# All tile arithmetic of GpSimd moved to VectorE in a planned transformer kernel

## The chip, the cores and the metric

The kernel runs on one core of one Trainium2 chip. The metric is the time of one execution in microseconds, the median of several executions; lower is better. A core has five engines that run side by side, each with its own queue of instructions in a fixed order: TensorE (PE, matrix products; its weight loads are shown apart as PEld), VectorE (DVE), ScalarE (ACT), GpSimd (POOL) and SyncE (SP, which here only issues transfers). They meet through semaphores alone.

## What is computed

Two layers over 512 tokens of width 1024, everything in float32. `rms` is a root-mean-square norm with a gain; each half layer is normed before and after ("sandwich").

```python
# layer 0
m = conformer_conv(rms(h))        # 1024 -> 2048, gate, causal depthwise conv of 31 taps,
                                  # layer norm, silu, 1024 -> 1024
h = h + rms(m)
h = h + rms(square(relu(rms(h) @ w_ff1)) @ w_ff2)       # 1024 -> 4096 -> 1024
# keys and values, once, from h
c_kv = rms(rms(h) @ w_dkv)                              # 256 wide
k_rope = rope(rms(h) @ w_kr)                            # 64 wide, shared by the heads
k_nope, v = c_kv @ w_uk, c_kv @ w_uv                    # 8 heads of 128
# layer 1
q = rms(rms(h) @ w_dq) @ w_uq                           # 384 wide -> 8 heads of 128 + 64
p = softmax((q_nope @ k_nope.T + rope(q_rope) @ k_rope.T) * scale + mask)   # chunks of 64
h = h + rms((p @ v) @ w_o)
h = h + rms(square(relu(rms(h) @ w_ff1)) @ w_ff2)
```

## The kernel before, in words

**Products in three parts.** The matrix products keep float32 accuracy with a rounded type. Each operand X is split into a main part `hi`, a rounded copy made by ScalarE, and a remainder `lo = X - hi`; a product is hi*hi + lo*hi + hi*lo. The remainder is one subtraction of two tiles. `split` does both steps, for weights (from tile `raw` into `wh` and `wl`) and for activations (into two tiles `big`). Some weights get their remainder by an accumulating transfer that GpSimd issues instead (`lo_by_dma`).

**Fast matrix algorithms.** The feed-forward parts use Winograd's and Strassen's forms with seven products in place of eight. `combinations` prepares what the seven products of the first matrix need: it first adds `hi` and `lo` of every half of the normed activations back together (16 additions of 128x256 a layer), then forms differences of them, then splits those again.

**Attention.** For every head: `keys`, `queries`, and for every pair of heads `values` and `rotary` project the latents with weights `uk`, `uq`, `uv`, `uqr` (those and `wo` are called `ATT`; their splits are listed in `VG`, that is, VectorE or GpSimd). `rotate` applies the rotary embedding: four copies by ScalarE, a product with the cosines on VectorE, then a product with the sines and a sum on GpSimd (and a further scaling for the key's part). `scores` does the products of queries and keys for one half of the query blocks, then on VectorE a masked maximum, on ScalarE the exponential with its sum, on VectorE a reciprocal and the scaling; `transposed` transposes the result on TensorE and splits it; `attend` multiplies by the values. TensorE's order runs one head ahead: while head n is attended, the projections and scores of head n+1 are issued (`PROJECTIONS` says which projections go after which half head).

**The planner.** No instruction is issued directly. `record` collects operations with the ways each may be done (an engine, a method, a price in ns from `cost`). TensorE's order is the order of the program text; for the others `due` works back from the end when each operation must be done, `schedule` simulates the engines and takes on each the operation that is due first among those that are ready, choosing between engines where an operation has several ways (`better`), and `replay` times the finished order once more. Sixteen rounds are tried and the shortest is issued, by `issue`, so in the profile nearly every instruction has the line L786 and is told from others by its tiles. The planner also knows a port: an operation marked `port` (two-input arithmetic of GpSimd, or of VectorE with more than one input outside PSUM) is not begun while another such is being done.

**Where a planned gap of TensorE is long, it inserts idle products** (`mm<-ident`, `bc<-ident`).

**GpSimd's work** is thus: memsets, the issue of accumulating and some other transfers, and the tile arithmetic that the change below moves. It has 233 instructions.

Of the kernel before, what the change touches and what calls it, by code (L numbers as in the profile page):

```python
# [8 lines left out]
F32 = mybir.dt.float32  # L9
F32R = mybir.dt.float32r  # L10
AF = mybir.ActivationFunctionType
ALU = mybir.AluOpType
# [11 lines left out]
H = 256  # L24
# [247 lines left out]


PORT = ("tensor_tensor", "scalar_tensor_tensor")

LEAD = 16000.0

# [46 lines left out]
class Program:  # L324
# [15 lines left out]
    def record(self, *ways):  # L340
        op = Op(len(self.ops))
        op.early = self.early
        self.ops.append(op)
        for engine, method, args, kwargs in ways:
            outs, ins = [], []
            for i, a in enumerate(args):
                if isinstance(a, View):
                    (outs if i == 0 else ins).append(a)
            for k, a in kwargs.items():
                if isinstance(a, View):  # L350
                    (outs if k in ("out", "accum_out") else ins).append(a)
            aps = [self.model(v) for v in outs], [self.model(v) for v in ins]
            if not op.ways:
                for write, views in ((False, ins), (True, outs)):
                    for view, ap in zip(views, aps[0 if write else 1]):
                        psum = ap.tensor.space == PSUM
                        self.touch(op, view.tile, write, _box(ap, ap.tensor.space != bass.MemoryType.SB), psum and engine)
            wide = [a for a in aps[1] if a.tensor.space != PSUM]
            op.port = method in PORT and engine in VG and (engine == "gpsimd" or len(wide) > 1)
            op.ways.append((engine, method, args, kwargs, self.cost(engine, method, kwargs, *aps), op.port))  # L360
        op.choose(op.ways[0])
        if op.method == "dma_start":
            self.flight(op)
        return op
# [28 lines left out]
    def cost(self, engine, method, kwargs, outs, ins):  # L393
        n = max([_size(a) for a in outs + ins] or [1])
        if method == "dma_start":
            return {"scalar": 380.0, "gpsimd": 900.0}.get(engine, 400.0)
        apart = {"vector": 0.77, "scalar": 0.6}.get(engine, 0.0) * n if any(
            list(a.ap)[-1][0] > 1 for a in outs + ins if _size(a) > 8
        ) else 0.0
        if engine in ("scalar", "vector") and ins and _size(ins[0]) > 8 and ins[0].ap[0][1] < P:  # L400
            apart += 120.0 if engine == "scalar" else 97.0
        if engine == "tensor":
            n = _size(outs[0])
            if ins[0].dtype == F32R:
                k = ins[0].ap[0][1]
                return max(120.0, n / 2.4 + 13.7) + (200.0 if k < P else 0.0)
            return 109.0 if method == "transpose" else max(222.0, n / 0.6 + 9)
        few = sum(_size(a) == 1 for a in ins) if n > 8 else 0
        psum = any(a.tensor.space == PSUM for a in outs + ins)
        if engine == "vector":  # L410
            wide = [a for a in ins if _size(a) > 1]
            rate = 1.042 if len(wide) > 1 or psum else 0.521
            return 68 + rate * n + 62 * few + apart
        if engine == "scalar" and n == 1:

            return 1350.0
        if engine == "scalar":
            few += "accum_out" in kwargs
            return (51 if psum else 94) + 0.833 * n + 93 * few + apart
        if engine == "gpsimd" and not ins:  # L420
            return 97 + 0.85 * n
        if engine == "gpsimd" and method == "affine_select":
            return 182 + 0.85 * n
        if engine == "gpsimd":
            return 150 + 2.1 * n
        return 450.0

    def flight(self, op):
# [236 lines left out]
    def replay(self, sequence, pace=1.0, add=0.0):  # L665
# [23 lines left out]
                for p in op.deps:  # L689
                    p.heirs.append(op)  # L690
        clock = dict.fromkeys(ENGINES, 570.0)
        port = 0.0
        coming, rings, since = [], {"sync": deque(), "scalar": deque(), "gpsimd": deque()}, 0.0

        def finish(op, at):
# [7 lines left out]
        while left or coming or any(rings.values()):  # L703
            best = None
            for e in ENGINES:
                if queue[e]:
                    op, way = queue[e][0]
                    if op is None:
                        t = clock[e]
                    elif op.open:  # L710
                        continue
                    else:
                        t = max(clock[e], op.free, port if way[5] else 0.0)
                    if best is None or t < best[0]:
                        best = t, e
            heads = [r[0] for r in rings.values() if r]
            turn = sum(j[2] for j in heads)
            done = since + min(j[1] for j in heads) * turn if heads else None
            come = coming[0][0] if coming else None
            event = min((x for x in (done, come) if x is not None), default=None)  # L720
            if event is not None and (best is None or event <= best[0]):
                for j in heads:
                    j[1] -= (event - since) / turn
                since = event
                for r in rings.values():
                    while r and r[0][1] < 1e-6:
                        j = r.popleft()
                        finish(j[0], event + LANDS[j[0].engine])
                while coming and coming[0][0] <= event:
                    _, _, e, j = heappop(coming)  # L730
                    rings[e].append(j)
                continue
            if best is None:
                raise RuntimeError("no order")
            now, e = best
            op, way = queue[e].popleft()
            left -= 1
            if op is None:
                clock[e] = now + FILL
                continue  # L740
            op.real = now
            clock[e] = now + way[4] * (1.88 if e == "tensor" and now < COLD else 1.0)
            if way[5]:
                port = clock[e]
            if "dma" in way[1]:
                heappush(coming, (now + STARTS[e], op.n, e, [op, op.packets, op.serve * pace + add]))
            else:
                finish(op, clock[e])
# [41 lines left out]
def trunk(ctx: ExitStack, tc: tile.TileContext, xT, xN, wts, vec, along, rope, cw, out):  # L790
# [123 lines left out]
    def weight(key):  # L914

        while key not in blocks:
# [23 lines left out]
            if i >= 4 and lo_by_dma(name):  # L940

                for o in range(0, n, 512):
                    for dst, scale in ((lo, -1.0), (hi, 1.0)):
                        nc.scalar.activation(dst[:, o : o + 512], raw[:, o : o + 512], AF.Copy, scale=scale)
                nc.gpsimd.dma_start(out=lo, in_=src, accum_op=ALU.add)
            else:
                step = 256 if i < 2 else min(n, 512)
                engines = VG if name[0] in ATT else ("vector",)
                for o in range(0, n, step):
                    split(raw, slice(o, o + step), (hi, lo), engines=engines)  # L950
            blocks[name] = hi, lo
# [197 lines left out]
    def combinations(X):  # L1149

        raw = {}
        for kh, th in QUADS:
            for kp in range(2):
                a = raw[kh, th, kp] = big()
                for j in range(2):
                    hi, lo = (x[:, th * H : (th + 1) * H].bitcast(F32) for x in X[4 * kh + 2 * kp + j])
                    nc.binary(("gpsimd", "vector"), out=a[:, j * H : (j + 1) * H], in0=hi, in1=lo, op=ALU.add)
        out = {p: [] for p in WINOGRAD}
        for k, (hi, lo) in enumerate(X):
            out[1 if k < 4 else 2].append((hi[:, :H], lo[:, :H]))  # L1160
# [513 lines left out]
    def rotate(pt, n, s, r=None):  # L1674
# [4 lines left out]
                nc.scalar.activation(b[x : x + 32, s], pt[y : y + 32, :n], AF.Copy)  # L1679
        rc, rs = (rope_c, rope_s) if r is None else (rope_cd, rope_sd)  # L1680
        nc.vector.tensor_tensor(out=a[:, s], in0=pt[:, :n], in1=rc[:, s], op=ALU.mult)
        nc.gpsimd.tensor_tensor(out=b[:, s], in0=b[:, s], in1=rs[:, s], op=ALU.mult)
        nc.gpsimd.tensor_tensor(out=a[:, s], in0=a[:, s], in1=b[:, s], op=ALU.add)
        if r is not None:
            nc.gpsimd.tensor_tensor(out=a[:, s], in0=a[:, s], in1=r[:, s], op=ALU.mult)
        return a


# [2 lines left out]
    def query_latent(m, t):  # L1691
# [8 lines left out]
        if m == 0:  # L1700
            nc.scalar.activation(undealt(qsq, t), src, AF.Square)
        else:
            sq = tmp()
            nc.scalar.activation(undealt(sq, t), src, AF.Square)
            qs = undealt(qsq, t)
            nc.binary(VG, out=qs, in0=qs, in1=undealt(sq, t), op=ALU.add)

    for t in (HA, HB):
        s = slice(t[0], t[0] + t[1])
# [47 lines left out]
    def rotary(pr):  # L1757

        a = rotate(products(("uqr", pr), CQ, 0, T, nk=3), T, ALL)
        for j in range(2):  # L1760
            q = QR[2 * pr + j] = big(F32R)
            mine, other = slice(64 * j, 64 * j + 64), slice(64 - 64 * j, 128 - 64 * j)
            nc.scalar.activation(q[mine], a[mine], AF.Copy)
            nc.binary(VG, out=q[other], in0=a[mine], in1=q[mine].bitcast(F32), op=ALU.subtract)

    def keys(hd):
        KN[hd] = pair()
# [225 lines left out]
```

## Time and profile before

| | |
|---|---|
| median of 3 executions | 1054.61 us (1054.33 to 1054.73) |
| the profiled execution | 1054.81 us, span 1052.6 us |
| TensorE busy, granted clock | 1032.1 us (98%), 0.997 |
| VectorE busy | 852.9 us (81%) |
| ScalarE busy | 679.0 us (65%) |
| GpSimd busy | 190.8 us (18%), its transfer issues included |

Times run from the first instruction of the span. A row of the grouped instructions gives line, engine, operation, output <- inputs, shape, count | busy us, mean ns of one | the engine's idle time ahead of them and who ended it. A row of the waits gives the waiting engine and tile, the one that released it, the total in us, the number of waits and the longest. A row of the timeline gives start, duration, engine, operation and, in brackets, the idle time before it. A row by stage gives the stretch, its length, then busy time and count of PE, PEld, DVE, ACT and POOL, the granted clock, the share of the transfer engines and GB/s. Matmul records overlap, as they are pipelined.

The stages by time: convolution layer to about 180 us, then the turn to the first feed-forward part (180 to 215), that part to about 535, latents and first projections to 567, the heads to 665, the output projection to 715, the turn to the second feed-forward part (715 to 740), and that part to the end.

### The profile page before, as it was taken

How to read it: one execution, taken by the hardware profiler on the slowest of the kernel's cores; microseconds unless marked ns; L12 is line 12 of the kernel's file. 1: busy time of each engine (PE TensorE's matmuls, PEld its weight loads, DVE VectorE, ACT ScalarE, POOL GpSimd, SP SyncE). 2: the span in 40 equal slices, each digit the busy share in tenths (PEclk: the TensorE clock that was granted, in tenths of full speed). 3: DMA queues.
4: the chain of work that ended last, by engine and by line, in shares of the span. 5: the costliest groups of instructions: out<-in, count | busy, mean ns of one | idle time of the engine just before them, and what ended most of it. 6: DMA issues, size and time to landing. Idle time of an engine off the chain costs nothing.

```text
span 1052.6 us, 16355 instructions
## 1 busy us (share of the span) xinstructions
PE 1032.1 (98%) x5750; PEld 897.3 (85%) x5750; DVE 852.9 (81%) x1657; ACT 679.0 (65%) x1351; POOL 190.8 (18%) x233
## 2 busy tenths in 40 slices
PE   8999999999999999999999999999999999999995
PEld 7888988899988888888898888889999878888884
DVE  6599994798999648859988977648989895497798
ACT  9462795877875546465767777558778764555652
POOL 1123201501011010101015443315010110000010
PEclk9999999999999999999999999999999999999998
DMA  9996997657899976769423210956588998766782
GB/s 321 308 230 174 355 291 180 140 140 172 269 280 295 268 200 204 193 182 251 99 86 102 66 68 1 347 153 141 141 205 262 297 298 258 195 200 166 209 211 80
DMA packets 67794, 211.50 MB, mean 201 GB/s; under 512 B 7936, under 2 KB 11648, under 8 KB 67712
## 3 DMA queue, kind: packets, MB, share of 16 engines
q1 hardware_dynamic: 50688, 151.20, 41.1%
q0 software_dynamic: 16304, 58.20, 29.4%
q10 hardware_dynamic: 720, 1.05, 0.3%
q8 instruction: 45, 0.74, 0.3%
q14 instruction: 37, 0.30, 0.1%
HBM read 204.92 MB, written 5.51 MB: 200 GB/s over the span
## 4 chain that ended last, share of the span: by engine, by line
PE 62%; DVE 14%; ACT 4%; issue 2%; DMA 0%; DVEq 0%; ACTq 0%
PE mm L786 61%; DVE big L786 8%; DVE wl L786 3%; PE bc L786 2%; ACT big L786 2%; DVE stat L786 1%; ACT wh L786 1%; DVE tmp L786 1%; ACT junk L786 1%; DVE raw L786 1%; DVE h L786 1%; DMA raw<-wts 0%; ACT wl L786 0%; ACT tmp L786 0%; DVEq L1989 0%
## 5 line engine op out<-in xcount | busy, mean ns | idle before, releaser
L786 PE MATMUL mm<-big,wh 128*128 128x256 f32 (+1 forms) x1800 | 442.0, 335 | 1.6 <-DVE big L786 1.1
L786 PE MATMUL mm<-wh,big 128*128 128x512 f32 (+1 forms) x1216 | 372.3, 385 | 0.0
L786 PEld LDWEIGHTS mm<-big,wh 128*128 128x128 f32 x1800 | 308.2, 190 | 36.4 <-ACT wh L786 1.7
L786 ACT ACTIVATE wh<-raw 128x512 fp32r<-128x512 f32 (+3 forms) x430 | 266.1, 663 | 77.0 <-PE mm L786 48.0
L786 PE MATMUL mm<-big,wl 128*128 128x256 f32 (+1 forms) x900 | 301.3, 336 | 0.6 <-DVE wl L786 0.5
L786 DVE TENSOR_TENSOR wl<-raw,wh 128x512 fp32r<-128x512 f32 (+3 forms) x335 | 234.5, 737 | 51.8 <-ACT wh L786 51.7
L786 PEld LDWEIGHTS mm<-wh,big 128*128 128x128 f32 x1216 | 226.0, 188 | 43.9 <-ACT wh L786 0.2
L786 PE MATMUL mm<-wl,big 128*128 128x512 f32 (+1 forms) x608 | 233.5, 385 | 1.1 <-DVE wl L786 1.1
L786 PEld LDWEIGHTS mm<-big,wl 128*128 128x128 f32 x900 | 170.8, 190 | 18.2 <-DVE wl L786 1.7
L786 DVE TENSOR_TENSOR big<-big,big 128x512 f32<-128x512 f32 (+4 forms) x167 | 109.0, 672 | 56.1 <-ACT big L786 37.8
L786 PEld LDWEIGHTS mm<-wl,big 128*128 128x128 f32 x608 | 114.2, 188 | 25.3 <-DVE wl L786 2.9
L786 POOL DMA_DIRECT2D raw<-wts x64 | 56.2, 883 | 428.9 <-DMA raw<-wts 134.3
L786 ACT ACTIVATE big<-tmp 128x512 fp32r<-128x512 f32 (+2 forms) x152 | 76.4, 525 | 56.0 <-DVE tmp L786 45.5
L786 ACT ACTIVATE big<-big 128x512 f32<-128x512 f32 (+4 forms) x152 | 83.3, 574 | 15.8 <-DVE big L786 13.1
L786 ACT ACTIVATE big<-mm 128x512 f32<-128x512 f32 (+5 forms) x126 | 64.8, 520 | 37.7 <-PE mm L786 35.9
L786 PE MATMUL mm<-big,big 128*128 128x256 f32 (+3 forms) x520 | 84.4, 310 | 0.5 <-ACT big L786 0.2
L786 PEld LDWEIGHTS mm<-big,big 128*128 128x128 f32 x520 | 72.8, 190 | 5.7 <-ACT big L786 1.2
L786 DVE TENSOR_TENSOR big<-big,mm 128x512 f32<-128x512 f32 x102 | 67.4, 682 | 11.4 <-PE mm L786 11.2
L786 POOL DMA_DIRECT2D wl<-wts x42 | 36.6, 872 | 218.5 <-ACT wl L786 189.1
L786 DVE TENSOR_TENSOR big<-tmp,big 128x512 fp32r<-128x512 f32 (+1 forms) x104 | 64.5, 624 | 6.5 <-ACT big L786 3.1
L786 ACT ACTIVATE tmp<-mm 128x512 f32<-128x512 f32 (+1 forms) x41 | 25.0, 609 | 68.5 <-PE mm L786 67.3
L786 DVE SCALAR_TENSOR_TENSOR big<-big,vt,big 128x512 fp32r<-128x512 f32 (+29 forms) x95 | 63.1, 731 | 5.6 <-ACT big L786 5.3
(93 smaller groups left out, 894.7 us busy)
## 6 DMA issues: line engine op xcount, KB each, us to landing
raw<-wts SPq DMA_DIRECT2D x224, 512.0 KB, 6.0
raw<-wts POOLq DMA_DIRECT2D x64, 512.0 KB, 8.7
wl<-wts POOLq DMA_DIRECT2D x42, 512.0 KB, 8.6
big<-cw SPq DMA_DIRECT2D x45, 256.0 KB, 6.5
big<-wts SPq DMA_DIRECT2D x12, 256.0 KB, 2.6
big<-along SPq DMA_DIRECT2D x10, 256.0 KB, 5.7
raw<-wts SPq DMA_DIRECT2D x12, 192.0 KB, 2.8
big<-xT SPq DMA_DIRECT2D x8, 256.0 KB, 4.4
```

What stands on the lines that cost most here:

```text
L786: return f(*args, **kwargs)
```

## The change

Every operation on tiles that GpSimd did or could do is given to VectorE alone: the additions in `combinations`, the remainders of attention weights in `weight`, the products and sums of `rotate`, the sum of squares in `query_latent` and the remainder of the rotated queries in `rotary`. The planner's prices for GpSimd, its rule of the port (which instructions hold it, and that a wait is only due when the other engine holds it) are changed as well.

```diff
+FAST = ("tensor_scalar", "tensor_copy")
...
             op.port = method in PORT and engine in VG and (engine == "gpsimd" or len(wide) > 1)
+            op.port |= method in FAST and engine == "vector" and len(wide) == len(aps[1]) and _size(aps[0][0]) > 64
...
         if engine == "gpsimd":
-            return 150 + 2.1 * n
+            return 235 + 2.2 * n
...
-        port = 0.0
+        port, held = 0.0, None
...
-                        t = max(clock[e], op.free, port if way[5] else 0.0)
+                        t = max(clock[e], op.free)
+                        if way[5] and held != e:
+                            t = max(t, port + 40.0 * (e == "vector"))
...
             if way[5]:
-                port = clock[e]
+                port, held = clock[e], e
...
-                engines = VG if name[0] in ATT else ("vector",)
+                engines = ("vector",)
...
-                    nc.binary(("gpsimd", "vector"), out=a[:, j * H : (j + 1) * H], in0=hi, in1=lo, op=ALU.add)
+                    nc.binary(("vector",), out=a[:, j * H : (j + 1) * H], in0=hi, in1=lo, op=ALU.add)
...
-        nc.gpsimd.tensor_tensor(out=b[:, s], in0=b[:, s], in1=rs[:, s], op=ALU.mult)
-        nc.gpsimd.tensor_tensor(out=a[:, s], in0=a[:, s], in1=b[:, s], op=ALU.add)
+        nc.vector.tensor_tensor(out=b[:, s], in0=b[:, s], in1=rs[:, s], op=ALU.mult)
+        nc.vector.tensor_tensor(out=a[:, s], in0=a[:, s], in1=b[:, s], op=ALU.add)
         if r is not None:
-            nc.gpsimd.tensor_tensor(out=a[:, s], in0=a[:, s], in1=r[:, s], op=ALU.mult)
+            nc.vector.tensor_tensor(out=a[:, s], in0=a[:, s], in1=r[:, s], op=ALU.mult)
...
-            nc.binary(VG, out=qs, in0=qs, in1=undealt(sq, t), op=ALU.add)
+            nc.binary(("vector",), out=qs, in0=qs, in1=undealt(sq, t), op=ALU.add)
...
-            nc.binary(VG, out=q[other], in0=a[mine], in1=q[mine].bitcast(F32), op=ALU.subtract)
+            nc.binary(("vector",), out=q[other], in0=a[mine], in1=q[mine].bitcast(F32), op=ALU.subtract)
```

## Prediction

> **What bounds the kernel now.** I read the page's first part, then the busy times by stage, then who waited for whom on the weight loads of TensorE, then the timeline where it waits.
>
> ```profile
> PE 1032.1 (98%) x5750; PEld 897.3 (85%) x5750; DVE 852.9 (81%) x1657; ACT 679.0 (65%) x1351; POOL 190.8 (18%) x233
> ```
>
> TensorE is the bound: 20.5 of 1052.6 us idle. The profiled execution took 1054.81 us (its span and 2.2 us around it), 0.2 us over the median of the runs, 1054.61; sums are made against 1054.8. A measurement of this kernel tells about 0.2% (2.1 us) from no change.
>
> Two answers by stage follow: the turns between layers (180 to 215 and 715 to 740), a stage of pure matrix products (215 to 340), attention over the heads (567 to 665.5), the output projection (665.5 to 715), and the end.
>
> ```profile
> 180.00:215.00 35.00, 33.64 (x243) 31.24 (x242) 28.50 (x61) 25.37 (x57) 15.25 (x19) 1.00 0.47 106
> 215.00:340.00 125.00, 125.00 (x804) 114.36 (x803) 116.41 (x187) 95.36 (x165) 16.45 (x19) 1.00 0.85 236
> ...
> 567.00:665.50 98.50, 95.16 (x566) 82.79 (x565) 82.29 (x241) 75.08 (x172) 38.65 (x34) 1.00 0.19 59
> 665.50:715.00 49.50, 49.50 (x239) 40.98 (x238) 23.81 (x48) 28.52 (x60) 12.03 (x12) 1.00 0.68 227
> 715.00:740.00 25.00, 24.68 (x207) 24.47 (x206) 23.95 (x52) 19.47 (x45) 11.18 (x16) 1.00 0.59 142
> ...
> 989.00:1040.00 51.00, 51.00 (x227) 42.23 (x226) 50.84 (x102) 28.00 (x57) 4.74 (x6) 1.00 0.65 171
> 1040.00:1052.60 12.60, 1.89 (x9) 1.23 (x7) 9.05 (x31) 1.63 (x4) 0.00 (x0) 0.75 0.33 125
> ```
>
> The columns are length, PE, PEld, DVE, ACT, POOL. PE has no gap in the long product stages, though VectorE is 93% busy there (116.4 of 125). Its gaps lie at the turns and in attention, which are the places where GpSimd computes. So a gain or a loss can only come from those; the end from 989 us on holds no tile arithmetic of GpSimd and moves along unchanged.
>
> Who ended the waits of the weight loads, by stage (attention; turn of layer 0; turn of layer 1). I take these rows for PE's stalls, since the ends of the matmuls themselves are modelled and hide part of a gap.
>
> ```profile
> PEld bc L786 <- DVE big L786: 4.5, 8, 0.8
> PEld bc L786 <- issue: 1.2, 1, 1.2
> ...
> PEld mm L786 <- DVE big L786: 1.3, 1, 1.3
> PEld bc L786 <- issue: 0.7, 2, 0.4
> ...
> PEld bc L786 <- issue: 0.5, 1, 0.5
> ```
>
> Attention 5.7 us, the turns 2.0 and 0.5. Why VectorE is late there shows in the timeline, once at the turn and once in attention:
>
> ```profile
> 190.22 3.13 POOL L786 TENSOR_TENSOR big<-big,big 128x256 f32<-128x256 f32 x4
> 191.68 2.23 DVE L786 TENSOR_TENSOR big<-big,big 128x512 f32<-128x512 f32 x1
> 194.96 0.30 PEld L786 LDWEIGHTS mm<-big,wh 128*128 128x128 f32 x2 [1.29 <-DVE big L786]
> ...
> 610.97 1.41 POOL L786 TENSOR_TENSOR big<-big,big 128x512 f32<-128x512 f32 x1
> 611.38 1.29 DVE L786 TENSOR_SCALAR big<-big,stat 128x512 f32<-128x512 f32 x1
> 612.72 0.20 PEld L786 LDWEIGHTS bc<-ident,big 128*128 128x128 f32 x2 [0.73 <-DVE big L786]
> ...
> 598.32 0.49 DVE L786 TENSOR_SCALAR big<-big,stat 128x512 f32<-128x512 f32 x1
> ```
>
> The same softmax scaling lasts 0.49 us alone and 1.29 us when a GpSimd instruction began before it; it ends when GpSimd does, and TensorE waits 0.73 us for it. The rows of the tiles say it of more instructions: minimum, median and maximum are
>
> ```profile
> L786 DVE SCALAR_TENSOR_TENSOR h<-big,stat,h x32: 740/746/2820, 182.9 to 1048.6; 128x512 f32<-128x512 f32 x32
> ...
> L786 DVE TENSOR_SCALAR big<-big,stat x32: 262/421/1461, 586.4 to 667.6; 128x128 f32<-128x128 f32 x8, 128x256 f32<-128x256 f32 x8, 128x384 f32<-128x384 f32 x8, 128x512 f32<-128x512 f32 x8
> ```
>
> **The change part by part.** It removes GpSimd's tile arithmetic and adds the same instructions to VectorE's queue. GpSimd keeps its DMA issues and memsets. The edits of the planner's prices and port rule have nothing left to act on, since every instruction that holds the port is then VectorE's own; but the planner searches the whole order anew, so instructions far from attention can also change places.
>
> *Price of one moved instruction.* What VectorE takes for the shapes in question:
>
> ```profile
> L786 DVE TENSOR_TENSOR big<-mm,big 128x256 fp32r<-128x256 f32 x16 | 6.3, 418 | 0.7 <-ACT big L786 0.6
> ...
> L786 DVE TENSOR_TENSOR big<-bc,big 128x384 fp32r<-128x384 f32 x16 | 8.7, 548 | 1.5 <-ACT big L786 1.4
> ...
> 478.85 1.20 DVE wl L786 x2
> ```
>
> In the chain two 512-wide remainders follow each other in 1.20 us, 0.60 apart; one alone lasts 0.685, so 0.08 overlaps with the next. I take 0.60, 0.47 and 0.34 us for 512, 384 and 256 columns.
>
> *The turns.* At 180 to 215 GpSimd does 15 sums of the convolution's halves for the Winograd-like combinations:
>
> ```profile
> L786 POOL TENSOR_TENSOR big<-big,big 128x256 f32<-128x256 f32 x15 | 12.6, 981 | 3.2 <-DVE big L786 1.6 <-DVE stat L786 1.5
> ```
>
> On VectorE 15 x 0.34 = 5.1 us. Against it stand the holds: the first add above 2.23 instead of 0.69, the longest of `h` 2.82 instead of 0.75; these two alone give 3.6 us back. VectorE's load, 28.5 of 35, thus rises by 1.5 us at most, and may fall. TensorE's stalls here go with their cause: 1.3 + 0.7. The turn of layer 1 has the same sums once more and 0.5. Together -2.2 us (0.3 of 2.5 kept as what is late next: the residual adds wait for ACT's sums of squares anyway). Bounds: -2.5 if all goes, 0 if the sums, now in VectorE's own queue, delay the adds as GpSimd did.
>
> *Attention.* What moves there:
>
> ```profile
> L786 POOL TENSOR_TENSOR big<-big,big 128x512 f32<-128x512 f32 x8 | 10.9, 1362 | 27.0 <-ACT big L786 26.7
> L786 POOL TENSOR_TENSOR wl<-raw,wh 128x512 fp32r<-128x512 f32 x7 | 9.1, 1309 | 12.7 <-ACT wh L786 10.3 <-issue 2.4
> L786 POOL TENSOR_TENSOR wl<-raw,wh 128x384 fp32r<-128x384 f32 x8 | 8.1, 1013 | 5.3 <-ACT wh L786 4.4 <-PE mm L786 0.8
> L786 POOL TENSOR_TENSOR big<-big,big 64x512 fp32r<-64x512 f32 x5 | 6.4, 1286 | 4.0 <-ACT big L786 2.8 <-issue 1.2
> L786 POOL TENSOR_TENSOR wl<-raw,wh 128x256 fp32r<-128x256 f32 x6 | 4.4, 736 | 7.5 <-ACT wh L786 5.3 <-PE bc L786 2.2
> ```
>
> 20 instructions of 512 columns x 0.60 + 8 x 0.47 + 6 x 0.34 = 17.8 us more for VectorE. What it gets back are the holds, by the stage's own rows:
>
> ```profile
> L786 DVE TENSOR_SCALAR big<-big,stat 128x512 f32<-128x512 f32 x7 | 5.5, 785 | 0.2
> ...
> L786 DVE TENSOR_SCALAR big<-big,stat 128x256 f32<-128x256 f32 x7 | 4.0, 570 | 0.1
> L786 DVE TENSOR_SCALAR big<-big,stat 128x384 f32<-128x384 f32 x7 | 3.9, 551 | 0.2
> L786 DVE TENSOR_SCALAR big<-big,stat 128x128 f32<-128x128 f32 x8 | 3.3, 408 | 0.2
> ...
> 582.11 1.41 DVE L786 SCALAR_TENSOR_TENSOR stat<-stat 128x4 f32<-128x4 f32 x2
> ```
>
> Free of holds, the smallest takes 0.262 (the minimum above) and the largest 0.49; between them 0.34 and 0.41. So 7 x 0.295 + 7 x 0.23 + 7 x 0.14 + 8 x 0.146 = 5.8, and 1.1 for the two tiny steps at 582 us (1.41 instead of two of 0.16): 6.9 us. VectorE then needs 82.3 + 17.8 - 6.9 = 93.2 us in a stage of 98.5, and TensorE 98.5 - 5.7 = 92.8. They come out level: VectorE joins TensorE as a bound. The stage's length is 93.2 divided by the share of it in which VectorE manages to work. Two rows bound that share: 93% (215 to 340) gives 100.2, a loss of 1.7; 99.7% (50.84 of 51, 989 to 1040) gives 93.5, a gain of 5.0. Neither is nearer in kind: attention has shorter dependencies than the first, less backlog than the second. I take the middle, 96.4%: 96.7, a gain of 1.8. What helps is that weight remainders are not urgent and can fill VectorE's gaps; what hurts is VectorE's queue in order: the idle columns of the rows above show some 50 us in which GpSimd sat waiting for ACT's first half, at no cost. On VectorE such a wait would stop the softmax steps queued behind it, for which TensorE waits.
>
> *The rest.* Before and after the heads' stage:
>
> ```profile
> 535.00:567.00 32.00, 32.00 (x240) 30.41 (x239) 26.04 (x66) 19.49 (x42) 13.38 (x13) 1.00 0.39 122
> ```
>
> ```profile
> L786 POOL TENSOR_TENSOR wl<-raw,wh 128x512 fp32r<-128x512 f32 x5 | 7.3, 1460 | 24.7 <-ACT wh L786 10.8 <-PE mm L786 7.9 <-DMA raw<-wts 5.9
> ```
>
> At 535 to 567 there are 13 instructions of 256 and 384 columns, at most 13 x 0.47 = 6.1 us; even without the holds given back that fills VectorE's 26.0 of 32 to the brim and no further, and PE has no gap there: 0, at worst +0.1. At 665.5 to 715 five remainders of `wo` are 3.0 us, covered by VectorE's 25.7 idle us; without that cover they would cost their 3.0. GpSimd's DMA issues come no later, since its queue only gets shorter: 0.
>
> Sum: 1054.8 - 2.2 - 1.8 = 1050.8 us.
>
> **The rivals.** *VectorE saturates in attention* (slower). Work taken from a third lane lands on the engine whose steps release every transpose. It decides where VectorE's share of the stage stays under 93.2 / (98.5 + 2.2 + 2.1) = 90.7%: slower by over 0.2% then. For it speaks today's share there, 83.6% (82.3 of 98.5); against it, that much of today's idle time is simply that nothing was due. At 90% the stage takes 103.6 and the kernel 1054.8 - 2.2 + 5.1 = 1057.7; at 83.6% it would be 111.5, and 1065.6.
> The Trainium skill has a rule for this side: Perfetto Trace Analysis, section Optimizing Scalar/DVE Operations, says that where VectorE is saturated, moving some work off it, even to GpSimd, may make sense, and adds that the two share a read port, so that it might not help. By its first half, with 93% as saturation, the sum would be 1054.3 in place of 1050.8; the holds in the rows above are its second half.
>
> *One wait replaces the other* (no change). PE's stall ends at the next latest step, a moved instruction or ACT (75 of 98.5 busy) instead of a hold. That is the share of 93%: 1054.8 - 2.2 + 1.7 = 1054.3.
>
> *All stalls go.* Share 99.7%: 1054.8 - 2.5 - 5.0 = 1047.3.
>
> *The order gets worse elsewhere.* The change would then not do only what it says: the new search could let a weight come late where PE waits for none today. What such lateness costs now, over the whole run, outside attention and the turns, is
>
> ```profile
> PEld mm L786 <- DVE wl L786: 4.6, 9, 0.9
> ```
>
> Half as much again would be +2.3: 1053.1 from the forecast. It lies within the widths and is no case of its own.
>
> **How the numbers follow.** Forecast 1050.8: 0.45. All stalls go, 1047.3: 0.12. No change, 1054.3: 0.20. Saturation, about 1057.7: 0.23. So faster 0.57, same 0.20, slower 0.23. The range, 1046 to 1058.5, takes in the best case with 1 us to spare and leaves out only saturation beyond 90%; the faster cases alone span 1046 to 1052.7.
>
> **What would show it.** Right: no VectorE scaling beyond about 0.5 us and no `h` update beyond 0.76 us; DVE's total near 853 + 10 + 18 + 9 moved - 7 - 7 held, some 876 us or less; PE's waits in attention below 4 us; the turns without the 1.3 us wait. The steps are wrong if `bc` weight loads wait on DVE as long as before although no hold is left (saturation), or if VectorE idles there waiting for ACT in front of moved remainders. The prediction fails most simply if attention grows beyond 101 us.

## The result and the profile after

The changed kernel takes 1046.15 us (median; 1045.86 to 1046.23) against 1054.61: ratio 0.992, 95% interval 0.9902 to 0.9937. It is 8.5 us faster, near the lower end of the forecast's range. The profiled execution has a span of 1044.2 us. From its page, busy time and share of the span:

```profile
PE 1030.3 (99%) x5738; PEld 896.9 (86%) x5738; DVE 856.7 (82%) x1739; ACT 677.6 (65%) x1351; POOL 108.8 (10%) x151
```

VectorE does 82 instructions more and is busy only 3.8 us longer. What had filled the place is in the rows of the tiles (minimum, median, maximum in ns): the scaling of the softmax and the residual update `h`.

```profile
L790 DVE TENSOR_SCALAR big<-big,stat x32: 268/380/481, 583.2 to 661.9; 128x128 f32<-128x128 f32 x8, 128x256 f32<-128x256 f32 x8, 128x384 f32<-128x384 f32 x8, 128x512 f32<-128x512 f32 x8
...
L790 DVE SCALAR_TENSOR_TENSOR h<-big,stat,h x32: 740/746/754, 183.7 to 1040.3; 128x512 f32<-128x512 f32 x32
```

The maxima were 1461 and 2820; the medians of `h` are the same. Neither is held any more. Busy time by stage (turn of layer 0, product stage, heads, output projection):

```profile
180.00:213.00 33.00, 33.00 (x237) 30.80 (x236) 30.60 (x81) 27.91 (x67) 3.46 (x4) 1.00 0.48 114
213.00:338.00 125.00, 125.00 (x808) 114.54 (x807) 113.94 (x184) 92.73 (x157) 16.02 (x19) 1.00 0.85 233
...
565.00:659.30 94.30, 93.89 (x569) 82.31 (x567) 88.66 (x274) 73.80 (x173) 0.00 (x0) 1.00 0.20 62
659.30:708.00 48.70, 48.70 (x235) 40.48 (x234) 25.21 (x58) 27.90 (x58) 3.46 (x4) 1.00 0.69 233
```

The heads take 94.3 us in place of 98.5, and VectorE is busy in 94% of them (88.66). Who ended the waits of the weight loads there, and in the turn of layer 0:

```profile
PEld bc L790 <- DVE big L790: 1.9, 8, 0.3
PEld bc L790 <- PE mm L790: 0.7, 1, 0.7
PEld mm L790 <- ACT big L790: 0.4, 2, 0.2
PEld bc L790 <- issue: 0.2, 1, 0.2
...
PEld bc L790 <- issue: 0.2, 1, 0.2
```

All rows of this view together, the waits in the heads were 6.8 us (the prediction counted the two longest rows, 5.7) and are now 3.2; of the turn's 2.0 remain 0.2.

**Where the time went.** TensorE issues the same 5686 products in all these kernels (idle products left out), but not quite in the same order: the planner's search moves TensorE's queue too, which is the order of the program text in the main only. By tiles and shapes, 693 of the 5686 places hold another product after than before. I compare when the k-th of them starts in two profiled executions; what that difference gains (minus) or loses (plus) over a stretch is the stretch's share. The last column is the change of the span. Stretches are named by the times of before.

| kernel (profiled execution) | to 180 | turn 180-215 | 215-510 | 510-567 | heads 567-666 | 666-740 (turn) | 740-1000 | end | sum |
|---|---|---|---|---|---|---|---|---|---|
| after | +0.75 | -1.70 | -1.24 | +0.09 | -4.39 | -0.47 | -0.84 | -0.54 | -8.34 |
| planner's rule alone | -0.39 | +0.09 | -1.57 | -0.58 | -1.47 | +2.21 | -1.17 | -1.00 | -3.88 |
| swap in place | +0.47 | -1.66 | +0.02 | -0.32 | +5.26 | +0.88 | +0.02 | +0.01 | +4.68 |
| order of after, GpSimd | +0.22 | -1.53 | -1.26 | +5.54 | -2.40 | +0.61 | -0.86 | -0.54 | -0.22 |
| fills for sums | +0.42 | -1.80 | -0.02 | -0.32 | -2.49 | -0.05 | -0.05 | +0.01 | -4.30 |
| turns only | +0.30 | -1.32 | -1.65 | -1.13 | -1.26 | -0.04 | -1.13 | -0.99 | -7.22 |
| heads only | +0.21 | -0.78 | -1.88 | +0.21 | -3.84 | +3.74 | -0.83 | -0.19 | -3.36 |
| doubled remainders | +0.51 | -1.69 | -1.34 | -0.36 | -2.03 | -0.59 | -0.84 | -0.92 | -7.26 |
| before, 32 rounds | +0.59 | -0.25 | +0.94 | +0.32 | -1.20 | +1.53 | -1.33 | -0.17 | +0.43 |
| shadow | +0.93 | +3.66 | -0.88 | +1.86 | +17.83 | +2.54 | -0.88 | +0.21 | +25.27 |

So the turns gave 2.2 us, the heads 4.4, and 2.6 came where GpSimd never did tile arithmetic (215-510, 740-1000, the end). The order of after on GpSimd has them as well (2.7), and the two kernels that keep the order of before have nothing there: they belong to the new order, not to the engine. The 0.75 lost at the start is no effect of the change: the swap in place, whose order is that of before, shows 0.47 there.

### The profile page after: what moved, and what is told of

Read it like the earlier page. It is cut to its first block, busy times and chain, and to the rows that moved or that the text cites. A ratio compares the mean times of both kernels' runs of the same rounds, so it can differ in the third digit from the quotient of the medians.

```text
span 1044.2 us, 16279 instructions
## 1 busy us (share of the span) xinstructions
PE 1030.3 (99%) x5738; PEld 896.9 (86%) x5738; DVE 856.7 (82%) x1739; ACT 677.6 (65%) x1351; POOL 108.8 (10%) x151
## 4 chain that ended last, share of the span: by engine, by line
PE 82%; DVE 11%; ACT 3%; issue 2%; DMA 1%; POOL 0%; DVEq 0%; ACTq 0%
PE mm L790 80%; DVE big L790 8%; ACT big L790 2%; PE bc L790 2%; DVE wl L790 2%; DVE stat L790 1%; DVE h L790 1%; DMA uu<-dealt 1%; ACT wh L790 0%; DMA vt<-vec 0%; ACT wl L790 0%; ACT tmp L790 0%; DVE tmp L790 0%; ACT junk L790 0%; POOL uu L790 0%
## 5 line engine op out<-in xcount | busy, mean ns | idle before, releaser
L790 DVE TENSOR_TENSOR wl<-raw,wh 128x512 fp32r<-128x512 f32 (+3 forms) x366 | 248.6, 711 | 67.3 <-ACT wh L790 65.5
L790 DVE TENSOR_TENSOR big<-big,big 128x512 f32<-128x512 f32 (+5 forms) x216 | 125.8, 610 | 43.2 <-ACT big L790 30.7
```

Source lines behind the costliest of these rows:

```text
L790: return f(*args, **kwargs)
```

## Experiments

Theory: the hold. VectorE stands still while a GpSimd instruction that began first runs, and TensorE waits for VectorE. Rivals: the order (the planner's new rule and new search), and the slow results of GpSimd. The trace of before speaks against the last: no wait of TensorE's weight loads or of VectorE ends with GpSimd's arithmetic, and ScalarE has one such wait.

```profile
ACT big L786 <- POOL big L786: 2.0, 1, 2.0
```

Medians, and ratios to runs of before on the same chip (1055.1 to 1055.3).

### Order and engine apart

*The planner's edits alone*, GpSimd keeping its work:

```diff
+            op.port |= method in FAST and engine == "vector" and len(wide) == len(aps[1]) and _size(aps[0][0]) > 64
...
-            return 150 + 2.1 * n
+            return 235 + 2.2 * n
...
-                        t = max(clock[e], op.free, port if way[5] else 0.0)
+                        t = max(clock[e], op.free)
+                        if way[5] and held != e:
+                            t = max(t, port + 40.0 * (e == "vector"))
```

> Only the planner's prices and port rule are changed; GpSimd keeps its arithmetic. Theory of the hold (VectorE stands still while a GpSimd instruction that began first runs, and TensorE waits for it): the holds stay, 1052 to 1056 us, scalings of 512 columns up to 1.3 us are still seen. Rival, the order (the new prices and the new search make the gain): 1046 to 1049.

1051.26 us, 0.9963 (0.9949 to 0.9977). Between the two readings. 1.5 us come off in the heads, where a planner that knows of the holds can avoid some, and 2.7 in the product stages, where there are none; the second turn loses 2.2. Holds remain: scalings last up to 1.22 us, and one `h` update 3.45. In the changed kernel these edits do nothing: built without them, it is the same program, instruction for instruction.

*Swap in place*:

```diff
         for op, (engine, method, args, kwargs, *_) in sequence:
+            if engine == "gpsimd" and method == "tensor_tensor":
+                engine = "vector"
```

> The order of before is kept on every engine; only at the issue does VectorE get each arithmetic instruction that was planned for GpSimd, at its place in the overall sequence. Hold: most of the gain comes without any new search, 1047.5 to 1051. Order: no gain, 1053.5 to 1058, since VectorE's queue was planned without these instructions. Latency (GpSimd's results come late because it is slower): 1047.5 to 1051 as under the hold, so this run does not part these two.

1059.21 us, 1.0038 (1.0025 to 1.005): slower than before. The turn still gains its 1.7 us, as the hold says, but the heads lose 5.3. Both theories had one half of it. What ScalarE and TensorE wait for there in this kernel:

```profile
ACT big L788 <- DVE stat L788: 15.8, 15, 3.5
...
PEld bc L788 <- DVE big L788: 6.8, 10, 1.8
```

In the changed kernel the first is

```profile
ACT big L790 <- DVE stat L790: 8.8, 9, 3.6
```

The exponentials wait for the maxima of the softmax. Moved instructions, placed by a plan that gave them to a free engine, now stand between the softmax's steps in VectorE's queue, which I take for the reason.

*The counterpart*: the planner's order for the changed kernel, with the moved instructions (marked as `moved` where they are recorded) issued on GpSimd. By the trace these are 94; in the kernel before GpSimd did 82, since the planner had given some to VectorE.

```diff
         for op, (engine, method, args, kwargs, *_) in sequence:
+            if op is not None and op.moved and method == "tensor_tensor":
+                engine = "gpsimd"
```

> The counterpart of the swap in place: the order that the planner found for the kernel after is kept, and each moved instruction is issued on GpSimd at its place in the overall sequence, all 80 or so. If the order alone made attention's gain: 1046 to 1049. If the engine must fit the order (the plan counts on 0.6 us and no hold where GpSimd takes 1.3 and holds VectorE): 1054 to 1064, the loss in attention and the turns.

1054.03 us, 0.9989 (0.998 to 0.9998): at the lowest edge of the second reading, far from the first. The loss lies at 510 to 567 (5.5 us), in the heads (2.0 us against after) and in the second turn (1.1), not in the first. At 556 to 562 us seven small steps on VectorE (`stat`) are each held by one of GpSimd's instructions, 0.43 to 0.70 us in place of 0.16, and TensorE waits 3.3 us for them:

```profile
PEld bc L793 <- DVE stat L793: 3.6, 2, 3.3
```

The four kernels make a square:

| | planned with GpSimd | planned with VectorE alone |
|---|---|---|
| arithmetic issued on GpSimd | 1054.6 | 1054.0 |
| arithmetic issued on VectorE | 1059.2 | 1046.15 |

Neither the engine nor the order alone brings the gain; each needs the other. (The corner on the right above has 12 instructions more on GpSimd than the one on the left.)

*The search by itself*: `rounds=16` becomes `rounds=32` in the kernel before.

> The kernel before, but the planner tries 32 rounds in place of 16 and so picks another order by its own forecast. It prices the search alone. If the gains of about 0.5 to 0.9 us each at 345, 505 and 867 us come from any new search: 1052 to 1053.5. If they need the change: 1054 to 1056, with those three waits as before.

1054.07 us, 0.9989 (0.998 to 0.9998), in the second reading's range. Another order moves single stretches by about 1 us either way (+0.94, -1.20, +1.53, -1.33) and the whole by 0.1%. So shares of that size outside the turns and heads can't be put down to the change.

### The hold

*Shadow*: the kernel after, and GpSimd repeats the moved instructions into a tile nobody reads: 92 by the trace, more than the 78 expected and the 82 of the kernel before.

```diff
+        if shade:
+            m = min(COLS, s.stop - s.start)
+            nc.shadow(
+                out=SHADOW[:, :m], in0=src[:, s.start : s.start + m],
+                in1=dst[0][:, d.start : d.start + m].bitcast(F32), op=ALU.subtract,
+            )
...
+                    nc.shadow(out=SHADOW[:, :m], in0=hi[:, :m], in1=lo[:, :m], op=ALU.add)
```

(and likewise behind the rotary products, their sums and remainders; `m` is the whole width here, 8 columns in the next run).

> The kernel after, and beside it GpSimd repeats 78 of the moved instructions, reading the same tiles, into a tile that nobody reads. No result of GpSimd is needed. Hold: VectorE's instructions are held again and VectorE has all its new work too: 1052 to 1058, 512-wide scalings of 1 us and more return, TensorE's weight loads wait over 4 us in attention. Latency and order: nothing changes, 1046 to 1047.5.

> As the run before, but each repeated instruction covers 8 columns, so it runs some 0.2 us in place of 0.7 to 1.3; places, waits and tile lifetimes are the same. Hold: the cost goes with the time held, so nearly all of the shadow's cost is gone, 1046 to 1048. If instead the longer lifetimes of the tiles or GpSimd's queue made the shadow's cost, this run is as slow as the shadow.

1079.81 us, 1.0231 (1.0217 to 1.0245) with full width, 1046.3, 0.9917 (0.9903 to 0.993) with 8 columns. The hold was expected, its size was not: 33.7 us for work whose results nobody needs, 18 of them in the heads against before (22 against after). The same 1739 instructions of VectorE are busy for 901.4 us in the full shadow and for 857.8 in the 8-column one. The timeline of the full shadow, and its stage of the heads:

```profile
606.85 4.39 POOL L795 TENSOR_TENSOR uu<-big,big 128x512 f32<-128x512 f32 x3 [13.13 <-DVE stat L795]
607.31 1.38 DVE L795 TENSOR_TENSOR big<-big,big 128x512 f32<-128x512 f32 x1
...
609.02 1.09 DVE L795 TENSOR_TENSOR wl<-raw,wh 128x256 fp32r<-128x256 f32 x1
...
572.70:689.50 116.80, 102.11 (x570) 86.43 (x568) 108.88 (x277) 75.03 (x172) 54.75 (x45) 0.96 0.20 65
```

VectorE's remainder of 256 columns lasts 1.09 us in place of 0.42, its rotary sum 1.38 in place of 0.69, while GpSimd runs three. Not all of the 22 us in the heads is the hold. TensorE's waits that end with VectorE are 16.6 us there against 1.9 after, so 14.7 more. One wait of 2.4 us is for a copy of a weight by ScalarE, which had shortly before waited 3.3 us for a tile that GpSimd still read. And the granted clock of the stage was 0.96 (0.77 at 605 to 620 us) in place of 1.00, some 4.7 us of 116.8 by my estimate from these two numbers. The 8-column run costs nothing, though GpSimd has as many instructions; it was planned anew (VectorE's order differs from the full shadow's in 549 of 1739 places) and frees its tiles sooner, so it does not part the time held from these by itself. The rows above do.

*Fills for sums*: the order of before; GpSimd writes zeros in place of its sums, products and remainders.

```diff
...
+            if engine == "gpsimd" and method == "tensor_tensor":
+                method, args, k = "memset", [k["out"].bitcast(F32), 0.0], {}
```

> The kernel before with its order on every engine; each arithmetic instruction of GpSimd is replaced at its place by a fill of the same output with zeros, which reads nothing (the sums, products and remainders that GpSimd made are left out). Hold by reading: VectorE's two-input instructions are no longer held, the turns lose their 1.3 us wait and attention some 2 to 4 us: 1049 to 1052. If any work of GpSimd on tiles holds VectorE, or if the slow results are what costs: 1053.5 to 1055.5.

1050.47 us, 0.9952 (0.994 to 0.9965): the hold by reading. The fills are also shorter (0.54 us on average for 512 columns into `wl`, in place of 1.37), so part of the gain can be GpSimd being done sooner; this run does not part the two in the heads. In the turns the rows do:

```profile
L786 DVE SCALAR_TENSOR_TENSOR h<-big,stat,h x32: 743/747/753, 183.4 to 1044.3; 128x512 f32<-128x512 f32 x32
```

The two-input `h` runs beside the fills unharmed (maximum 753 ns, before 2820; at 202.2 us one runs beside six of them). The one-input scaling does not:

```profile
637.85 0.52 POOL L786 MEMSET big<- 64x512 f32 x1 [3.14 <-PE bc L786]
637.87 2.99 DVE L786 TENSOR_SCALAR big<-big,stat 128x256 f32<-128x256 f32 x1
638.32 2.39 POOL L786 MEMSET wl<- 128x512 f32 x5
```

It lasts 2.99 us in place of 0.35, through six fills in a row.
The Trainium skill (SBUF — State Buffer, Who interferes with whom) has this difference: two SBUF inputs on VectorE collide only with a GpSimd instruction that reads, while a `tensor_scalar` in a two-port mode collides with any. Both halves agree with the rows above; that the scaling ran in that mode is not shown by itself.

### The parts

*Turns only* (the planner's edits, and only the sums on VectorE) and *heads only* (everything but the sums):

```diff
-                    nc.binary(("gpsimd", "vector"), out=a[:, j * H : (j + 1) * H], in0=hi, in1=lo, op=ALU.add)
+                    nc.binary(("vector",), out=a[:, j * H : (j + 1) * H], in0=hi, in1=lo, op=ALU.add)
```

> The planner's new rule, and only the 32 sums of the combinations on VectorE; attention's arithmetic stays with GpSimd. The run with the planner's rule alone took 1051.3. Hold in the turns: 2.0 to 2.5 us come off, 1048.5 to 1049.8, and the 1.3 us wait of the weight loads at 195 us is gone. If all that is left of the gain lies in attention: 1051 to 1052.

> All of the change but the sums of the combinations, which GpSimd may still take. The turns' part of about 2.2 us is given back, attention keeps its gain: 1047.5 to 1049.5. If the turns brought nothing: 1046 to 1046.8.

1046.98, 0.9924 (0.9911 to 0.9936), and 1051.39, 0.9966 (0.9954 to 0.9979). Both missed: the turns' part is worth 4.3 us on top of the planner's edits and costs 5.2 when given back, twice what was expected. With the sums alone moved, GpSimd still does 41 instructions of tile arithmetic and scalings still last up to 1.24 us; yet the kernel is 0.8 us slower than the changed one, inside the measurement. Its heads are 3.1 us longer, but the rest of its order is shorter by 2.0. So moving the arithmetic of attention is not shown to be worth anything on the whole beyond the sums and the planner's rule. Why giving the sums back costs so much shows in the timeline of heads only, at the second turn:

```profile
714.50 5.76 DVE L790 SCALAR_TENSOR_TENSOR h<-big,stat,h 128x512 f32<-128x512 f32 x3
715.26 3.78 POOL L790 TENSOR_TENSOR big<-big,big 128x256 f32<-128x256 f32 x5
...
719.65 1.14 PEld L790 LDWEIGHTS bc<-ident,h 128*128 128x128 f32 x6 [2.83 <-DVE h L790]
```

Three updates of `h` take 5.76 us in place of 2.1, as one of them (4.43 us) waits for five sums in a row, and TensorE waits 2.83 us. In before the sums happened to be placed better here (0.5 us). What a hold costs is a matter of where it falls.

*Rotary on GpSimd*: the kernel after, with `nc.vector` back to `nc.gpsimd` in the last three lines of `rotate`.

> The kernel after, with the products and sums of the rotary embedding back on GpSimd (14 instructions), all else on VectorE. If a hold costs wherever it falls: 1047.5 to 1050, with scalings over 1 us again. If attention has room for these holds because the planner knows of them: 1046 to 1047.

1049.19 us, 0.9935 (0.9923 to 0.9947); the heads gain 0.8 us instead of 4.4. The scalings, expected over 1 us, are not held (490 ns at most); the planner's rule covers them. A remainder is:

```profile
585.73 1.30 POOL L790 TENSOR_TENSOR big<-big,big 128x512 f32<-128x512 f32 x1 [12.03 <-ACT big L790]
585.76 1.55 DVE L790 TENSOR_TENSOR wl<-raw,wh 128x256 fp32r<-128x256 f32 x1
...
588.56 0.31 PEld L790 LDWEIGHTS bc<-ident,big 128*128 128x128 f32 x3 [1.38 <-DVE big L790]
```

It began 0.03 us after GpSimd and lasts 1.55 us in place of 0.42; the softmax steps behind it come late by that much.

### Is VectorE the bound of the heads now?

*Doubled remainders* (each of the weights' remainders of the heads computed twice), and the scaling free to go to ScalarE:

```diff
+                    if name[0] in ATT[:4]:
+                        nc.binary(engines, out=lo[:, o : o + step], in0=raw[:, o : o + step], in1=hi[:, o : o + step].bitcast(F32), op=ALU.subtract)
```

```diff
-            nc.vector.tensor_scalar(out=S[:, ks], in0=S[:, ks], scalar1=st[:, 3:4], scalar2=None, op0=ALU.mult)
+            nc.record(
+                ("vector", "tensor_scalar", (), dict(out=S[:, ks], in0=S[:, ks], scalar1=st[:, 3:4], scalar2=None, op0=ALU.mult)),
+                ("scalar", "activation", (S[:, ks], S[:, ks], AF.Copy), dict(scale=st[:, 3:4])),
+            )
```

> The kernel after, with the remainder of each of the weights uq, uqr, uk and uv computed twice by VectorE (some 10 us more for it, most in the heads' stage, where it was busy 88.7 of 94.3 us). If VectorE is now the bound there: 1050 to 1054, slower by what does not fit. If TensorE is, and VectorE's gaps can be filled: 1046 to 1048.

> The kernel after, with the scaling of the softmax free to go to ScalarE where the planner finds that better (17 of 32 go). If VectorE is the bound in attention: 1043.5 to 1045.5. If not, or if ScalarE's 0.5 us for each lie on the same chain: 1046 to 1048.

1047.26, 0.9927 (0.9915 to 0.9939), and 1046.28, 0.9916 (0.9903 to 0.993). With more load the kernel takes 1.1 us more, inside the measurement; less load brings nothing. The heads with the doubled remainders:

```profile
564.00:660.00 96.00, 94.78 (x564) 81.91 (x564) 94.65 (x286) 73.30 (x170) 0.00 (x0) 1.00 0.18 58
```

VectorE is busy 94.65 of 96.0 us, 98.6%, and the stage is 2.4 us longer than after by the table (-2.03 against -4.39). Of 6.0 us more of work in the stage (94.65 against 88.66), 3.6 went into VectorE's gaps and 2.4 did not. So VectorE is not the bound of the changed kernel, but it is near it. No run beat the changed kernel beyond the measurement.

## Why the prediction came out as it did

**The mechanism was right.** GpSimd's instructions hold VectorE, TensorE waits for that, and with the work moved the holds are gone; the rows of held instructions, the shadow and, in the turns, the fills show it. It is one part of the gain: 2.6 us are the new order's, and the heads gain nothing from the change of engine without that order (the swap in place).

**The turns were right**: forecast -2.2, measured -1.70 and -0.47. VectorE's load rose from 28.5 of 35 to 30.6 of 33, by 2.1 us where the prediction gave 1.5 as the most, at no cost.

**The heads were mis-sized**: forecast -1.8, measured -4.4. Two figures of that step failed. VectorE's need was put at 93.2 us and was 88.7. The sum added durations to a busy time in which neighbouring records overlap, less 0.08 for each of 34 moved instructions, 2.7. The traces part the 4.5 us: the durations of VectorE's records in the stage add up to 94.9 before and 106.9 after, 12.0 more, and the busy time rose by 6.4, so 5.6 more overlap. That is 2.9 beyond the 2.7; the other 1.6 are durations (13.6 more were expected), as a few other instructions fell outside the stage in the new order. Then the share of the stage in which VectorE can work was taken as 96.4%, the middle between 93 and 99.7. The doubled remainders reach 98.6%. At 88.7 us of need VectorE sets nothing, and the stage's length of 94.3 lies 1.5 over the 92.8 that the prediction gave TensorE alone (91.7, if all 6.8 us of its waits are taken off). The price of the queue in order, which I had set against it, is real: it is what the swap in place pays, 5.3 us. The new search avoids it.

**The rest was wrong in its sign.** "The rest" was put at 0, and the sentence on a worse order left out that the order could get better where nothing moved. 2.6 us came from there. The step that a gain can only come from the turns and attention rested on a row in which TensorE is busy throughout (215 to 340); the weight loads' waits at 215 to 510 were 1.6 us and at 740 to 1000 1.3, and are now 1.2 and 0.8. The planner's edits alone show 3.7 in the same three stretches; a mere re-search gains 0.6 there. Why a planner that reckons less with GpSimd does better in stages without GpSimd's arithmetic is not settled.

**The rivals.** Saturation did not happen: 94% in the heads, no cost at this load. Its condition was a good one: the swap in place has the same work on VectorE, VectorE is busy in 87.6% of its heads (91.06 of 104.0 us), under the 90.7%, and it is 4.0 us slower than before on its chip. What the prediction cites from the Trainium skill (Perfetto Trace Analysis, Optimizing Scalar/DVE Operations), that with a saturated VectorE moving some work to GpSimd may make sense, is not borne out here: with the order of after, handing the work back costs 7.9 us. But at 94% VectorE was not quite saturated, and the same section warns that such a move might not help. The case "all stalls go", 1047.3, came nearest, but by another sum: stalls of 3.2 us remain in the heads, and the search's gains stand in for them. Of the signs named for being right, all came: no scaling beyond 0.48 us, no `h` beyond 0.754, waits of 3.2 us in attention, no wait of 1.3 in the turn; VectorE's total of "some 876 us or less" fits loosely (856.7).

## To carry to other kernels

Before a second engine is given arithmetic beside VectorE, look at the maximum, not the mean, of VectorE's instructions: the same shape at 0.49 and 1.29 us is a hold, and it counts as busy time, so a moved instruction can cost less than its own length. A change of engine and the order that was planned for it belong together: here the engine alone lost 0.4%, the order alone gained 0.1%, and both gained 0.8%. A planner that knows of the holds gained 0.4% with the work left where it was, and 0.8% with only the urgent sums moved. When a planner re-searches the whole program, price the search itself by a run, and expect some 1 to 1.5 us a stretch of it in either direction.

## What the runs showed of the hardware

I had expected a hold to last as long as one GpSimd instruction. At times it lasted through a whole run of them: one `h` update through five sums (4.43 us in place of 0.75, heads only), one scaling through six fills (2.99 us in place of 0.35), though other sums and fills ended in between. At other times VectorE came in after each: in the full shadow's timeline the two held instructions end at 608.69 and 610.11 us, among GpSimd's three, and in the order of after on GpSimd the seven small steps and GpSimd's instructions take turns. What decides between the two, these runs do not show.

The hold works the other way too. In the 8-column shadow, GpSimd's instructions are (minimum, median, maximum in ns)

```profile
L795 POOL TENSOR_TENSOR uu<-big,big x52: 194/202/20636, 190.6 to 744.3; 128x8 f32<-128x8 f32 x44, 64x8 f32<-64x8 f32 x8
```

The one of 20.6 us begins at 723.6 us, lasts through 35 instructions of VectorE with two inputs in SBUF, one right behind another, and ends when one with an input in PSUM follows (`big<-tmp,mm`, 744.1 us). GpSimd's spans are rough in this profile, but its next instruction comes only then. Such waits lie inside an instruction's own duration and not in the wait for a semaphore, so "they meet through semaphores alone", as the opening has it, is too narrow.

And fills, which read nothing, hold a one-input scaling (2.99 us) but not a two-input update (753 ns at most).
